# Queueing the resident w2 loads behind the streamed loads, holding eight normalised MLP tiles, and loading the first pair's w1 among the transposes

## Chip, core and metric

The kernel runs on one NeuronCore of one Trainium2 chip. The metric is the device time of one execution in microseconds (us). A matmul instruction here multiplies a 128x128 stationary tile by a 128x512 moving tile; TensorE is called PE, VectorE DVE, ScalarE ACT, GpSimd POOL, and SyncE, which issues the DMAs that matter here, SP.

## Reference

One layer of a hybrid encoder block on x of 1024 tokens by 1024 channels in float32. Only its last part is touched by the change:

```python
x = x + mix @ w_out                                   # 1024x1024
h2 = rms_norm(x, norm_mlp)
x = x + jnp.square(jax.nn.relu(h2 @ w_ff1)) @ w_ff2   # w_ff1 1024x4096, w_ff2 4096x1024
return rms_norm(x, norm_final)
```

## The kernel before

Each float32 factor is split into a high part (ACT casts it, names ending in hi) and the remainder (DVE subtracts, names ending in lo), and a product is three matmuls, hi by hi, hi by lo and lo by hi (`mm3`, L114). Both MLP products use a seven-product scheme of Strassen's kind: the operands are cut into quarters, sums of quarters are formed, and seven products of half size replace eight. The scheme's left operands have the names A11, A12, A22, S1, S2, S3, S4.

The order of the work around the change is this.

**The w_out stage** (L755 to L805). The 8 token tiles are taken in 4 pairs. A pair has four PSUM accumulators `pw` (two tiles, two column halves) of 24 matmuls each; the first pair runs over all four accumulators for each of the 8 row tiles of w_out, the later pairs finish one accumulator after the other. There are four PSUM banks with this tag, so a pair takes the banks of the pair before it. For each token tile DVE adds the accumulator to the residual `x2`, ACT squares the sum and adds up (`square_sum`, L111), POOL raises to the power -1/2 (`rstd`, L108), and DVE scales `x2` into the normalised tile `hn` (L786). The square's elementwise output is written into `hn` and never read. `hn` has 6 buffers for 8 tiles. The `x2` tiles are also stored to DRAM (`x2_d`, L783).

**The transposes.** Tiles 0 to 3 are transposed on PE into `h2t` (L137). Tiles 4 to 7 are combined with tiles 0 to 3 into four `parts` of five operands (L799 to L805), which `transpose_parts` (L815) transposes, four 128x128 blocks each, into PSUM tiles `pt`; ACT and DVE split each of them into `s_hi` and `s_lo`. Among the transposes, `ff1_lead` (L887) does the first two products for column pairs 0, 1 and 2 of w_ff1, since they need `h2t` alone.

**The first MLP product**, 16 pairs g (`ff1`, L892): each loads two blocks of w_ff1 (`raw`), POOL forms four differences from them (`ta`, `tb`), ACT and DVE split them, PE does seven products of 12 matmuls, and the results are combined, squared and stored to DRAM as seven operands (`aops`).

**The second MLP product**, seven products (`product2`, L983) of 16 steps k with 12 matmuls each, in the order A12, A11, S1, S2, S3, A22, S4. A step loads its left operand from DRAM (the streamed load, L992) and its part of w_ff2 by `b_of`. For A12 and A22 that part is streamed as well; for A11, S1 and S2 it goes into resident tiles `r1`, `r2`, `r3` (48 loads of 256 KB, L975), which later products reuse after a subtraction on DVE.

The order of instructions on each engine is chosen by the framework's scheduler; the program can add edges to it. `issue_after(ins)` adds an edge to `ins` from each instruction in its block that runs on the same engine as `ins`:

```python
with tc.issue_after(steps[-1 - AHEAD]) if len(steps) > AHEAD else nullcontext():   # L993
    b = b_of(k, raw[:, 1])
...
    steps[-1] = nc.scalar.copy(out=hi[:, 0], in_=raw[:, 0]).ins                    # L1001, on ACT
```

Here `steps` holds casts on ACT, while `b_of` issues DMAs on SP and subtractions on DVE.

Of the kernel before, what the change touches and what calls it, by code (L numbers as in the profile page):

```python
# [8 lines left out]
F32 = mybir.dt.float32  # L9
# [38 lines left out]
def hybrid_block_kernel(ctx, tc, x, norm_mix, w_in, w_gate_up, b_gate_up, gla_norm, w_proj_sb, w_proj_gla,  # L48
# [717 lines left out]
    for t2 in range(NT // 2):  # L766
# [10 lines left out]
        for tt in (2 * t2, 2 * t2 + 1):  # L777
            hn = hp.tile([P, D], F32, tag="hn", name="hn", bufs=6)
            sums = small.tile([P, 2], F32, tag="ss2", name="sums")
            for ch, sl in enumerate(col_halves):  # L780
                add(x2[tt][:, sl], accs[(tt % 2) * 2 + ch], x2[tt][:, sl])
                square_sum(hn[:, sl], x2[tt][:, sl], sums[:, ch:ch + 1], D)
            nc.sync.dma_start(out=x2_d[tt], in_=x2[tt])  # L783
            r = rstd_of(sums, 2)
            for ch, sl in enumerate(col_halves):
                nc.vector.scalar_tensor_tensor(out=hn[:, sl], in0=x2[tt][:, sl], scalar=r, in1=g_mlp[ch],  # L786
                                               op0=ALU.mult, op1=ALU.mult)
            hns.append(hn)
            if tt < 4:
                load_x2(tt + 4)  # L790
        if t2 == 1:
            ha, hb = (big.tile([P, 4, KT, P], F32R, tag=f"big_{t}0", name=f"h2t_{t}") for t in ("hi", "lo"))
            for tt in range(4):
                transpose_hl((hns[tt][:, c_lo], hns[tt][:, c_hi]),
                             lambda kg: (ha[:, tt, kg * 4:kg * 4 + 4, :], hb[:, tt, kg * 4:kg * 4 + 4, :]), ("tr", "fill"), 2)
        for tt in range(2 * t2, 2 * t2 + 2):
            if tt < 4:
                continue
            h0, h1 = hns[tt - 4], hns[tt]  # L799
            st = hp.tile([P, D], F32, tag="st", name="st", bufs=2)  # L800
            add(st[:, c_lo], h1[:, c_lo], h1[:, c_hi])
            sub(st[:, c_hi], st[:, c_lo], h0[:, c_lo])
            sub(h0[:, c_lo], h0[:, c_lo], h1[:, c_lo], nc.gpsimd)
            sub(h0[:, c_hi], h0[:, c_hi], st[:, c_hi])
            parts.append((st[:, c_hi], h0[:, c_lo], st[:, c_lo], h1[:, c_hi], h0[:, c_hi]))  # L805
# [86 lines left out]
    def ff1(g):  # L892
# [8 lines left out]
        def temp(tag, pool, shape=(P, HALF), bufs=1):  # L901
            return pool.tile(list(shape), F32, tag=tag, name=tag, bufs=bufs)
# [7 lines left out]
        c = lead[g] if g < LEAD else ff1_first(g, pair((b11, b21)))  # L910
# [3 lines left out]
        ta = temp("ta", sop, (P, 2, 4, P))  # L914
        sub(ta[:, 1], b12, b11, nc.gpsimd)
        sub(ta[:, 0], b22, ta[:, 1], nc.gpsimd)
        t2_, t1_ = pair((ta,))
        tb = temp("tb", sop, (P, 2, 4, P))
        sub(tb[:, 0], b22, b12, nc.gpsimd)
        sub(tb[:, 1], b21, ta[:, 0], nc.gpsimd)  # L920
        add(u2, product(t2_, "S2"), u2)
        pc = product(t1_, "S1")
        p5 = temp("p5", sop)
# [3 lines left out]
        u3 = temp("u3", sop)  # L927
# [15 lines left out]
        s2 = temp("s2", fp, bufs=2)  # L943
# [5 lines left out]
        s4 = temp("s4", fp)  # L949
# [5 lines left out]
    transpose_parts((0, 1))  # L955
    ff1_lead(1)
# [22 lines left out]
    AHEAD = 4  # L979
    n_ring = 0  # L980
    steps = []

    def product2(n, o, b_of, tail=False):  # L983
# [3 lines left out]
        for k in range(NK):  # L987
            steps.append(None)
# [3 lines left out]
            nc.sync.dma_start(out=raw[:, 0], in_=aops[o][k])  # L992
            with tc.issue_after(steps[-1 - AHEAD]) if len(steps) > AHEAD else nullcontext():  # L993
                b = b_of(k, raw[:, 1])
            hi = pool.tile([P, 2, HALF], F32R, tag="whi", name="whi", bufs=2)
            lo = pool.tile([P, 2, HALF], F32R, tag="wlo", name="wlo", bufs=2)
            if b is None:
                steps[-1] = nc.scalar.copy(out=hi, in_=raw).ins  # L998
                sub(lo, raw, hi.bitcast(F32))
            else:  # L1000
                steps[-1] = nc.scalar.copy(out=hi[:, 0], in_=raw[:, 0]).ins  # L1001
# [45 lines left out]
    u, v = (xf.tile([P, 4, HALF], F32, name=t) for t in ("u", "v"))  # L1047
# [22 lines left out]
    for i in range(4):  # L1070
        nc.scalar.copy(out=u[:, i], in_=p1[i])
# [7 lines left out]
    for i in range(4):  # L1079
        add(u[:, i], p6[i], u[:, i])  # L1080
        add(x3[i][:, c_hi], u[:, i], x3[i][:, c_hi])
    g_fin = load_g(norm_final)
    p7 = product2(4, "S3", t3x)
    for i in range(4):
        add(u[:, i], p7[i], u[:, i])
        add(v[:, i], u[:, i], v[:, i])
        for sl, src in ((c_hi, v), (c_lo, u)):
            add(x3[4 + i][:, sl], src[:, i], x3[4 + i][:, sl])
# [51 lines left out]
```

## Time and profile before

| what | value |
|---|---|
| median of 3 runs | 1714.35 us (1713.69 to 1715.68) |
| the profiled execution, its own time | 1714.85 us |
| its span in the profile | 1713.1 us |
| PE busy | 1654.5 us (97%) |
| DVE, ACT, POOL busy | 1147.2, 760.5, 388.9 us |
| moved by DMA | 193.54 MB, mean 113 GB/s |
| mean granted PE clock | 0.988 of 2.4 GHz |

The profile shows one execution. Its timeline lists instructions of an engine with start and duration, both in us; a bracket gives how long the engine was idle before and what ended that wait. Durations of matmuls overlap, since they are pipelined, so the pace is read from start to start. The windows view gives, for stretches of time, the busy time of the engines with the count of instructions, the granted PE clock (1.00 is 2.4 GHz), the mean busy share of the 16 DMA engines and their GB/s. In the DMA queue's timeline (SPq) a row is a run of issues by one line.

### The profile page before, as it was taken

The page shows a single profiled execution, that of the slowest core. Times are in us where ns is not written, and L with a number is a line of the kernel's source. Part 1 is how long each engine was busy: PE and PEld are TensorE (multiplying, and loading weights), DVE is VectorE, ACT ScalarE, POOL GpSimd, SP SyncE. Part 2 cuts the span into 40 slices and gives each one's busy share as a digit, 9 for nine tenths or more (in the row PEclk, how much of TensorE's full clock was granted, in tenths as well). Part 3 has the DMA queues.
Part 4 walks back from the last instruction along what each step waited for, and adds up shares of the span by engine and source line. Part 5 has one row for each costly group of instructions (what it writes and reads, how often), then busy time and mean ns, then how long its engine had stood idle before and what let it go on. Part 6 is the DMA issues. An engine that isn't in the chain of part 4 may idle for free.

```text
span 1713.1 us, 22677 instructions
## 1 busy us (share of the span) xinstructions
PE 1654.5 (97%) x8160; PEld 1380.8 (81%) x8160; DVE 1147.2 (67%) x1951; ACT 760.5 (44%) x1545; POOL 388.9 (23%) x380
## 2 busy tenths in 40 slices
PE   7999999999999999999999999899999987999997
PEld 5788888888898888788887787688888866888886
DVE  7678576674624878778856545787776646965695
ACT  6556454564424656557554313222222224444454
POOL 4010000000010121111110011797777520000061
PEclk9999999999999999999999999999999998999999
DMA  7003013032111110116336621454444596333453
GB/s 213 25 20 109 27 49 94 19 91 70 31 62 50 56 54 16 41 58 185 105 130 220 228 79 62 137 164 160 142 142 161 176 389 232 98 98 94 136 166 128
DMA packets 152912, 193.54 MB, mean 113 GB/s; under 512 B 11696, under 2 KB 90544, under 8 KB 152800
## 3 DMA queue, kind: packets, MB, share of 16 engines
q1 hardware_dynamic: 149424, 189.31, 34.6%
q10 hardware_dynamic: 3376, 2.79, 0.5%
q8 instruction: 64, 1.05, 0.3%
q14 instruction: 48, 0.39, 0.1%
HBM read 137.53 MB, written 54.53 MB: 112 GB/s over the span
## 4 chain that ended last, share of the span: by engine, by line
PE 85%; DMA 7%; DVE 4%; ACT 2%; issue 1%; POOL 1%; SPq 0%; ACTq 0%; POOLq 0%; DVEq 0%
PE mmt L115 7%; PE mmt L117 7%; PE mmt L116 7%; PE pq L115 6%; PE pq L116 6%; PE pq L117 6%; PE pp L116 5%; PE pp L115 5%; PE pp L117 5%; PE mmn L116 4%; PE mmn L117 4%; PE mmn L115 4%; PE sc L408 2%; DMA r<-in_w_ff_dram 2%; PE pw L115 2%; PE pw L117 2%
## 5 line engine op out<-in xcount | busy, mean ns | idle before, releaser
L117 PE MATMUL mmt<-ht_hi,wlo 128*128 128x512 f32 x512 | 201.4, 393 | 2.7 <-DVE wlo L79 2.7
L115 PE MATMUL mmt<-ht_hi,whi 128*128 128x512 f32 x512 | 201.6, 394 | 1.3 <-DVE qs L543 1.3
L116 PE MATMUL mmt<-ht_lo,whi 128*128 128x512 f32 x512 | 201.1, 393 | 0.0
L108 POOL TENSOR_TENSOR rstd<-ms,mhalf 128x1 f32<-128x1 f32 x56 | 43.1, 773 | 637.4 <-DVE ms L104 420.4
L115 PE MATMUL pp<-whi 128*128 128x512 f32 x448 | 164.2, 393 | 15.2 <-ACT whi L998 15.2
L116 PE MATMUL pp<-wlo,whi 128*128 128x512 f32 x448 | 176.6, 394 | 0.2
L117 PE MATMUL pp<-whi,wlo 128*128 128x512 f32 x448 | 175.4, 392 | 0.0
L749 DVE TENSOR_TENSOR wlo<-raw,whi 128x512 fp32r<-128x512 f32 (+1 forms) x112 | 89.0, 795 | 96.8 <-ACT whi L1001 53.9
L79 DVE TENSOR_TENSOR wlo<-raw,whi 128x1024 fp32r<-128x1024 f32 (+1 forms) x111 | 122.2, 1102 | 43.8 <-ACT whi L76 43.3
L76 ACT CAST whi<-raw 128x1024 fp32r<-128x1024 f32 (+1 forms) x113 | 95.9, 860 | 114.4 <-PE pq L116 34.7
L116 PE MATMUL mmn<-wlo,ht_hi 128*128 128x512 f32 (+1 forms) x384 | 138.8, 362 | 1.9 <-POOL wlo L79 1.5
L115 PE MATMUL mmn<-whi,ht_hi 128*128 128x512 f32 (+1 forms) x384 | 139.3, 364 | 0.4 <-DVE kl L558 0.4
L117 PE MATMUL mmn<-whi,ht_lo 128*128 128x512 f32 (+1 forms) x384 | 138.6, 361 | 0.0
L115 PE MATMUL pq<-s_hi,whi 128*128 128x512 f32 x320 | 127.4, 398 | 6.6 <-ACT whi L76 6.6
L116 PE MATMUL pq<-s_lo,whi 128*128 128x512 f32 x320 | 126.4, 395 | 0.0
L117 PE MATMUL pq<-s_hi,wlo 128*128 128x512 f32 x320 | 126.2, 395 | 0.0
L1001 ACT CAST whi<-raw 128x512 fp32r<-128x512 f32 x96 | 59.8, 623 | 134.0 <-PE pp L117 110.8
L117 PEld LDWEIGHTS mmt<-ht_hi,wlo 128*128 128x128 f32 x512 | 96.2, 188 | 22.0 <-DVE wlo L79 3.3
L115 PEld LDWEIGHTS mmt<-ht_hi,whi 128*128 128x128 f32 x512 | 96.3, 188 | 20.0 <-issue 1.7
L115 PEld LDWEIGHTS pp<-whi 128*128 128x128 f32 x448 | 84.1, 189 | 34.8 <-ACT whi L998 17.5
L116 PEld LDWEIGHTS mmt<-ht_lo,whi 128*128 128x128 f32 x512 | 96.3, 188 | 18.6
L116 PEld LDWEIGHTS pp<-wlo,whi 128*128 128x128 f32 x448 | 85.0, 190 | 20.2 <-DVE wlo L749 2.7
(261 smaller groups left out, 4024.2 us busy)
## 6 DMA issues: line engine op xcount, KB each, us to landing
raw<-in_w_in_dram SPq DMA_DIRECT2D x36, 512.0 KB, 4.0
raw<-in_w_ff_dram SPq DMA_DIRECT2D x35, 512.0 KB, 4.3
raw<-aop_S SPq DMA_DIRECT2D x64, 256.0 KB, 2.6
aop_A<-c SPq DMA_DIRECT2D x48, 256.0 KB, 3.0
aop_S<-s SPq DMA_DIRECT2D x48, 256.0 KB, 2.2
raw<-aop_A SPq DMA_DIRECT2D x48, 256.0 KB, 2.8
r<-in_w_ff_dram SPq DMA_DIRECT2D x48, 256.0 KB, 5.4
raw<-in_w_in_dram SPq DMA_DIRECT2D x32, 256.0 KB, 3.4
```

The source lines that it names most:

```text
L76: nc.scalar.copy(out=hi, in_=src)
L79: lo_eng.tensor_tensor(out=lo, in0=src, in1=hi.bitcast(F32), op=ALU.subtract)
L108: rstd_ins.append(nc.gpsimd.tensor_tensor(out=r, in0=ms, in1=mhalf, op=ALU.pow).ins)
L115: nc.tensor.matmul(ps, lhsT=sh, rhs=mh, start=first, stop=False)
L116: nc.tensor.matmul(ps, lhsT=sh, rhs=ml, start=False, stop=False)
L117: nc.tensor.matmul(ps, lhsT=sl, rhs=mh, start=False, stop=last)
L408: nc.tensor.matmul(sc[:P - H, i * 64:(i + 1) * 64], lhsT=lev[H][:, j, :P - H], rhs=right, start=True, stop=True)
L749: eng.tensor_tensor(out=out, in0=in0, in1=in1, op=ALU.subtract)
L1001: steps[-1] = nc.scalar.copy(out=hi[:, 0], in_=raw[:, 0]).ins
```

## The change

It has three parts.

1. In `product2` the block around `b_of` is now queued behind the streamed load of the same step, which is on SP.
2. All eight normalised tiles are held at once, in other places: tiles 0, 1, 4, 5 in `hn` (4 buffers), tiles 2 and 3 in the buffers `a21` and `s1` of the pool `fp`, which is opened earlier, and tiles 6 and 7 in `x2` itself, in place, after its store. The squares are written into the accumulators `pw` instead of `hn`. The five operands of a part are formed with three subtractions and one addition that overwrite their inputs, with different engines. The tile `u` of the second product moves into `fp` too.
3. The loads and the weight differences of a pair are a function of their own (`ff1_prep`), and that of pair 0 stands after the transposes of parts 0 and 1; the pool `hp` is closed there, and the second pool of load buffers (`s2`) is opened there.

```diff
+    fp = ctx.enter_context(tc.tile_pool(name="fp", bufs=1))
...
+    def norm_tiles(tt):
+        if tt >= 6:
+            return [x2[tt][:, sl] for sl in col_halves]
+        if tt in (2, 3):
+            return [fp_half("a21"), fp_half("s1")]
+        hn = hp.tile([P, D], F32, tag="hn", name="hn", bufs=4)
+        return [hn[:, sl] for sl in col_halves]
...
-            hn = hp.tile([P, D], F32, tag="hn", name="hn", bufs=6)
             sums = small.tile([P, 2], F32, tag="ss2", name="sums")
             for ch, sl in enumerate(col_halves):
                 add(x2[tt][:, sl], accs[(tt % 2) * 2 + ch], x2[tt][:, sl])
-                square_sum(hn[:, sl], x2[tt][:, sl], sums[:, ch:ch + 1], D)
+                square_sum(accs[(tt % 2) * 2 + ch], x2[tt][:, sl], sums[:, ch:ch + 1], D)
+            hn = norm_tiles(tt)
             nc.sync.dma_start(out=x2_d[tt], in_=x2[tt])
...
-            st = hp.tile([P, D], F32, tag="st", name="st", bufs=2)
-            add(st[:, c_lo], h1[:, c_lo], h1[:, c_hi])
-            sub(st[:, c_hi], st[:, c_lo], h0[:, c_lo])
-            sub(h0[:, c_lo], h0[:, c_lo], h1[:, c_lo], nc.gpsimd)
-            sub(h0[:, c_hi], h0[:, c_hi], st[:, c_hi])
+            st = hp.tile([P, HALF], F32, tag="st", name="st", bufs=2) if tt < 6 else fp_half("s2")
+            sub(h0[0], h0[0], h1[0])
+            sub(st, h1[1], h0[0])
+            add(h1[0], h1[0], h1[1], nc.vector if tt < 6 else nc.gpsimd)
+            sub(h0[1], h0[1], st)
...
+    def ff1_prep(g):
         raw = []
         for kh in range(2):
             raw.append(ring([P, 4, 2 * P], F32, "raw"))
...
+        w1 = pair((b11, b21)) if g >= LEAD else None
+        ta = temp("ta", (P, 2, 4, P))
+        sub(ta[:, 1], b12, b11, nc.gpsimd)
+        sub(ta[:, 0], b22, ta[:, 1], nc.gpsimd)
+        wt = pair((ta,))
+        tb = temp("tb", (P, 2, 4, P))
+        sub(tb[:, 0], b22, b12, nc.gpsimd)
+        sub(tb[:, 1], b21, ta[:, 0], nc.gpsimd)
+        return w1, wt, tb, b22
...
     ff1_lead(0)
     transpose_parts((0, 1))
+    hp_stack.close()
+    pools2.append(ctx.enter_context(tc.tile_pool(name="s2", bufs=1)))
+    n_st = [1, 1]
+    ready = ff1_prep(0)
     ff1_lead(1)
     transpose_parts((2,))
     ff1_lead(2)
     transpose_parts((3,))
-    hp_stack.close()
-    pools2.append(ctx.enter_context(tc.tile_pool(name="s2", bufs=1)))
-    with tc.tile_pool(name="fp", bufs=1) as fp:
-        for g in range(NF // 2):
-            ff1(g)
+    for g in range(NF // 2):
+        ff1(g, *(ready if g == 0 else ff1_prep(g)))
...
-            nc.sync.dma_start(out=raw[:, 0], in_=aops[o][k])
-            with tc.issue_after(steps[-1 - AHEAD]) if len(steps) > AHEAD else nullcontext():
+            load = nc.sync.dma_start(out=raw[:, 0], in_=aops[o][k]).ins
+            with tc.issue_after(load):
                 b = b_of(k, raw[:, 1])
```

What this does to the order, at three places. **The first** is SP's queue in the second MLP product. Before, in the middle of the product A12 (`raw<-aop` and `raw<-in_w_ff` are the two streamed loads of a step, `r` the resident ones, `x` a reload of the residual):

```order
L992 DMA raw<-aop_A_10281 128x512
L975 DMA raw<-in_w_ff_dram 128x512
L975 DMA r_12861<-in_w_ff_dram 128x512 x5
L975 DMA r_12862<-in_w_ff_dram 128x512 x8
L975 DMA r_12863<-in_w_ff_dram 128x512 x4
L992 DMA raw<-aop_A_10281 128x512
L975 DMA raw<-in_w_ff_dram 128x512
L975 DMA r_12863<-in_w_ff_dram 128x512 x3
```

Now, at the end of A12 and the beginning of A11:

```order
L1007 DMA raw<-aop_A_10284 128x512
L993 DMA raw<-in_w_ff_dram 128x512
L1007 DMA raw<-aop_A_10283 128x512
L993 DMA r_12857<-in_w_ff_dram 128x512
L1007 DMA raw<-aop_A_10283 128x512
L993 DMA r_12857<-in_w_ff_dram 128x512
```

All 48 resident loads stood among the steps of A12 and the end of the first MLP product; now each stands right behind the streamed load of its own step in A11, S1 or S2.

The eight reloads of the residual (512 KB each, `x`), which `b_of` issues too, have moved in the same way, from A12 into A11 and S3.

**The second** is the first pair of the w_out stage, on ACT, and the matmul on PE that opens the first accumulator of the second pair. ACT before (`whi<-raw` splits the first two blocks of w_ff1):

```order
L76 CAST wo_hi_9661<-raw 128x1024 [waits DMAHW3_49]
L76 CAST whi<-raw 128x1024 [waits DMAHW2_49]
L112 ACTIVATE hn,sums<-x_0_9665 128x512 [waits DMAHW4_49,DVE_49]
L76 CAST whi<-raw 128x1024 [waits DMAHW3_49]
L112 ACTIVATE hn,sums<-x_0_9665 128x512 [waits DVE_49]
```

ACT now:

```order
L76 CAST wo_hi_9664<-raw 128x1024 [waits DMAHW3_49]
L76 CAST whi<-raw 128x1024 [waits DMAHW2_49]
L112 ACTIVATE pw,sums<-x_0_9668 128x512 [waits DMAHW4_49,DVE_49]
L112 ACTIVATE pw,sums<-x_0_9668 128x512 [waits DVE_49]
L112 ACTIVATE pw,sums<-x_1_9670 128x512 [waits DMAHW5_49,DVE_49]
L112 ACTIVATE pw,sums<-x_1_9670 128x512 [waits DVE_49]
L76 CAST whi<-raw 128x1024 [waits DMAHW5_49]
```

PE before, the last matmuls of the first pair and the first of the second:

```order
L115 MATMUL pw<-wo_hi_9661,mixt_hi_8921 128x512
L116 MATMUL pw<-wo_lo_9662,mixt_hi_8921 128x512
L117 MATMUL pw<-wo_hi_9661,mixt_lo_8922 128x512
L115 MATMUL pw<-wo_hi_9312,mixt_hi_8921 128x512 [waits DVE_49]
L116 MATMUL pw<-wo_lo_9313,mixt_hi_8921 128x512
```

PE now:

```order
L115 MATMUL pw<-wo_hi_9664,mixt_hi_8921 128x512
L116 MATMUL pw<-wo_lo_9665,mixt_hi_8921 128x512
L117 MATMUL pw<-wo_hi_9664,mixt_lo_8922 128x512
L115 MATMUL pw<-wo_hi_9312,mixt_hi_8921 128x512 [waits Activation_49]
L116 MATMUL pw<-wo_lo_9313,mixt_hi_8921 128x512
```

The cast of the first w_ff1 block stands ahead of the first square in both. The matmul waits for ACT's square where it waited for DVE's addition.

**The third** is PE between the w_out stage and the first pair's own products (`pq<-s`), with the names of the transposed tiles. Before, from the end of the last product of column pair 2 on:

```order
L115 MATMUL pq<-h2t_hi,whi 128x512
L116 MATMUL pq<-h2t_lo,whi 128x512
L117 MATMUL pq<-h2t_hi,wlo 128x512
L822 MATMUL pt<-ident,st 128x128 x4
L822 MATMUL pt<-ident,hn 128x128 x4
L822 MATMUL pt<-ident,st 128x128 x4
L822 MATMUL pt<-ident,hn 128x128 x8
L115 MATMUL pq<-s_hi,whi 128x512
```

Now, around the beginning of the products of column pair 2:

```order
L835 MATMUL pt<-ident,x_6_9924 128x128 x8
L835 MATMUL pt<-ident,s_9916 128x128 x4
L835 MATMUL pt<-ident,s_10265 128x128 x4
L835 MATMUL pt<-ident,x_7_9940 128x128 x4
L115 MATMUL pq<-h2t_hi,whi 128x512
L116 MATMUL pq<-h2t_lo,whi 128x512
L115 MATMUL pq<-h2t_hi,whi 128x512
L116 MATMUL pq<-h2t_lo,whi 128x512
L835 MATMUL pt<-ident,a_9931 128x128 x4
L115 MATMUL pq<-s_hi,whi 128x512
```

The products of column pair 2 (24 matmuls) now stand between the last transposes and the first pair's products, where before five transposes stood directly ahead of them.

## Rows read from the trace of the kernel before

**Rows 1.** Timeline of PE: the waits between the w_out stage and the end.

```profile
1058.37 0.66 PE L822 MATMUL pt<-ident,hn 128*128 128x128 f32 x4 [1.53 <-DVE s_lo L749]
1061.22 1.12 PE L822 MATMUL pt<-ident,hn 128*128 128x128 f32 x4 [2.20 <-DVE s_lo L749]
...
1082.19 0.79 PE L115 MATMUL pq<-s_hi,whi 128*128 128x512 f32 x1 [6.57 <-ACT whi L76]
...
1417.24 2.08 PE L115 MATMUL pp<-whi 128*128 128x512 f32 x4 [10.26 <-ACT whi L998]
...
1430.34 1.25 PE L115 MATMUL pp<-whi 128*128 128x512 f32 x4 [3.82 <-ACT whi L998]
```

**Rows 2.** Timeline of ACT in product A12.

```profile
1416.14 1.04 ACT L998 CAST whi<-raw 128x1024 fp32r<-128x1024 f32 x1 [12.58 <-DMA raw<-in_w_ff_dram]
```

**Rows 3.** Timeline of the DMA queue SPq in product A12.

```profile
1397.70 11.51 SPq L975 DMA_DIRECT2D r<-in_w_ff_dram  x17
1410.03 0.33 SPq L992 DMA_DIRECT2D raw<-aop_A  x1
1410.66 0.33 SPq L975 DMA_DIRECT2D raw<-in_w_ff_dram  x1
```

**Rows 4.** Windows of PE in A12: stretch, length, busy, clock, DMA share, GB/s.

```profile
1377.70:1394.00 16.30, 16.30 (x73) 1.00 1.05 395
1394.00:1437.70 43.70, 28.28 (x98) 0.84 0.97 355
```

**Rows 5.** Timeline of PE: first matmul of A12, and two later steps of it.

```profile
1377.76 0.40 PE L115 MATMUL pp<-whi 128*128 128x512 f32 x1
...
1434.99 1.07 PE L115 MATMUL pp<-whi 128*128 128x512 f32 x4
...
1437.71 1.07 PE L115 MATMUL pp<-whi 128*128 128x512 f32 x4
```

**Rows 6.** Windows, in A11/S1 and during A22's loads: busy of five engines, clock, DMA share, GB/s.

```profile
1450.00:1500.00 50.00, 50.00 (x222) 41.43 (x221) 47.64 (x77) 22.53 (x40) 0.00 (x0) 1.00 0.34 95
...
1600.00:1650.00 50.00, 50.00 (x222) 41.42 (x221) 44.56 (x67) 23.13 (x44) 24.06 (x4) 1.00 0.53 174
```

**Rows 7.** Timelines around the second pair of the w_out stage: PE, DVE, ACT.

```profile
971.51 0.39 PE L115 MATMUL pw<-wo_hi,mixt_hi 128*128 128x512 f32 x1
...
982.91 0.69 DVE L746 TENSOR_TENSOR x<-pw,x 128x512 f32<-128x512 f32 x1 [0.38 <-PE pw L117]
...
973.82 1.05 ACT L76 CAST whi<-raw 128x1024 fp32r<-128x1024 f32 x1 [8.55 <-DMA raw<-in_w_ff_dram]
974.77 0.63 ACT L112 ACTIVATE hn<-x 128x512 f32<-128x512 f32 x1
```

**Rows 8.** Timeline of PE after the w_out stage.

```profile
1042.19 0.39 PE L115 MATMUL pq<-h2t_hi,whi 128*128 128x512 f32 x1
...
1047.66 0.60 PE L822 MATMUL pt<-ident,st 128*128 128x128 f32 x4
1048.10 0.60 PE L822 MATMUL pt<-ident,hn 128*128 128x128 f32 x4
...
1086.85 0.40 PE L115 MATMUL pq<-s_hi,whi 128*128 128x512 f32 x1
```

**Rows 9.** Timeline of DVE, same place.

```profile
1042.39 0.69 DVE L746 TENSOR_TENSOR x<-pw,x 128x512 f32<-128x512 f32 x1 [4.91 <-PE pw L117]
...
1074.22 3.08 DVE L749 TENSOR_TENSOR s_lo<-pt,s_hi 128x512 fp32r<-128x512 f32 x5
```

**Rows 10.** Timelines of SPq and of POOL, same place.

```profile
1075.77 23.15 SPq L896 DMA_DIRECT2D raw<-in_w_ff_dram  x6
...
1079.80 1.26 POOL L749 TENSOR_TENSOR ta<-raw,ta 128x512 f32<-128x512 f32 x1 [12.57 <-DMA raw<-in_w_ff_dram]
...
1089.67 2.28 POOL L749 TENSOR_TENSOR tb<-raw,ta 128x512 f32<-128x512 f32 x1
```

**Rows 11.** The line L783, stores of x2: time from issue to landing.

```profile
DMA to landing us min/median/max: 2.6/2.9/5.6
```

More of the change, by code (lines that the diff above doesn't have):

```diff
@@ L1 @@
-from contextlib import ExitStack, nullcontext
+from contextlib import ExitStack
 import concourse.bass as bass
@@ L785, in hybrid_block_kernel @@
             for ch, sl in enumerate(col_halves):
-                nc.vector.scalar_tensor_tensor(out=hn[:, sl], in0=x2[tt][:, sl], scalar=r, in1=g_mlp[ch],
+                nc.vector.scalar_tensor_tensor(out=hn[ch], in0=x2[tt][:, sl], scalar=r, in1=g_mlp[ch],
                                                op0=ALU.mult, op1=ALU.mult)
@@ L799, in hybrid_block_kernel @@
             h0, h1 = hns[tt - 4], hns[tt]
[L800 to L805 removed]
+            st = hp.tile([P, HALF], F32, tag="st", name="st", bufs=2) if tt < 6 else fp_half("s2")
[3 more added lines that the diff above has]
+            sub(h0[1], h0[1], st)
+            parts.append((st, h0[0], h1[0], h1[1], h0[1]))
     wo_stack.close()
@@ L890, in ff1_lead, with temp @@
         lead.append(ff1_first(g, pair((raw,))))
-    def ff1(g):
+    def temp(tag, shape=(P, HALF)):
+        return sop.tile(list(shape), F32, tag=tag, name=tag)
+    def ff1_prep(g):
         raw = []
@@ L899, in ff1 @@
         b21, b22 = raw[1][:, :, :P], raw[1][:, :, P:]
-        def temp(tag, pool, shape=(P, HALF), bufs=1):
-            return pool.tile(list(shape), F32, tag=tag, name=tag, bufs=bufs)
+        w1 = pair((b11, b21)) if g >= LEAD else None
[7 more added lines that the diff above has]
+        return w1, wt, tb, b22
+    def ff1(g, w1, wt, tb, b22):
         def relu_sq(c):
@@ L908, in store @@
             nc.sync.dma_start(out=aops[o][g], in_=c)
-        c = lead[g] if g < LEAD else ff1_first(g, pair((b11, b21)))
+        c = lead[g] if g < LEAD else ff1_first(g, w1)
         a11, u2 = c[:, 0], c[:, 1]
@@ L913, in ff1 @@
         store("A11", a11)
[L914 to L923, printed above, removed]
+        add(u2, product(wt[0], "S2"), u2)
+        pc = product(wt[1], "S1")
+        p5 = temp("p5")
         nc.scalar.copy(out=p5, in_=pc)
@@ L997, in product2 @@
             if b is None:
-                steps[-1] = nc.scalar.copy(out=hi, in_=raw).ins
+                nc.scalar.copy(out=hi, in_=raw)
                 sub(lo, raw, hi.bitcast(F32))
             else:
-                steps[-1] = nc.scalar.copy(out=hi[:, 0], in_=raw[:, 0]).ins
+                nc.scalar.copy(out=hi[:, 0], in_=raw[:, 0])
                 sub(lo[:, 0], raw[:, 0], hi[:, 0].bitcast(F32))
@@ L1045, in t4 @@
         return at(r1, k)
-    u, v = (xf.tile([P, 4, HALF], F32, name=t) for t in ("u", "v"))
+    u = [fp_half(t) for t in ("a21", "s1") for _ in range(2)]
+    v = xf.tile([P, 4, HALF], F32, name="v")
     xh = xf.tile([P, 4, D], F32, name="x3_0")
@@ L1070, in hybrid_block_kernel @@
     for i in range(4):
-        nc.scalar.copy(out=u[:, i], in_=p1[i])
+        nc.scalar.copy(out=u[i], in_=p1[i])
         add(v[:, i], p1[i], v[:, i])
@@ L1079, in hybrid_block_kernel @@
     for i in range(4):
-        add(u[:, i], p6[i], u[:, i])
-        add(x3[i][:, c_hi], u[:, i], x3[i][:, c_hi])
+        add(u[i], p6[i], u[i])
+        add(x3[i][:, c_hi], u[i], x3[i][:, c_hi])
     g_fin = load_g(norm_final)
@@ L1084, in hybrid_block_kernel @@
     for i in range(4):
[L1085 to L1088, printed above, removed]
+        add(u[i], p7[i], u[i])
+        add(v[:, i], u[i], v[:, i])
+        for sl, src in ((c_hi, v[:, i]), (c_lo, u[i])):
+            add(x3[4 + i][:, sl], src, x3[4 + i][:, sl])
     def finish(tt, acc, ch):
```

19 lines of the change are left out of this document (9 added, 10 removed).

## Prediction

> **What bounds the kernel now.** PE is busy 97% of the span, so I looked first, in the list of who waited for whom, at the little that PE waits. PE's timeline puts nearly all of it in two places [rows 1]. Between the w_out stage and the first MLP product there are waits of 1.53, 2.20 and 6.57 us (and two of 0.4); in the product A12 there are waits of 10.26 and 3.82 us (and one of 1.1). The reader should see that the gaps are few and large, and that everything between them is PE at full clock. A change elsewhere gains nothing unless it lets PE start something sooner.
>
> In A12 the chain goes PE, ACT, DMA. PE waits for the cast `whi`; ACT's row at 1416.14 says that ACT had itself waited 12.58 us for `raw<-in_w_ff` [rows 2]; and the queue shows why that load was late: SP issued 17 resident loads from 1397.70 on, and only then, at 1410.03 and 1410.66, the next streamed pair [rows 3]. Meanwhile the DMA engines were full, 395 and 355 GB/s at a busy share near 1 [rows 4]. So a stretch of traffic that nobody needs yet holds up traffic that PE needs now.
>
> At the first place PE's 6.57 us end with the cast of `ta`. POOL had waited 12.57 us for the load of w_ff1 [rows 10], which SP could issue only at 1075.77, when the last transposes had freed its memory.
>
> **Resident loads (part 1): a gain of 21.0 us.** A step of A12 is 12 matmuls and takes 2.72 us at full pace (1434.99 to 1437.71) [rows 5]. The step that begins at 1437.71 is the fifteenth: the windows count 73 + 98 = 171 matmuls from 1377.70 to 1437.70 [rows 4], 14 steps of 12 and a few that straddle an edge. Fourteen steps after 1377.76 would end at 1415.8; they end 21.9 us later. Of this 15.2 us are the three waits, the rest matmuls at the lower clock (0.84 granted on average [rows 4]) and weights that come just in time. With the 17 loads gone each step needs two loads of 256 KB in 2.72 us, 193 GB/s, half of what was moved here. I take 21.0 and keep 0.9 for first steps that may come late. The bounds are 21.9 and, if a third wait like the 3.82 us stays, 18.
>
> The loads do not vanish. A11, S1 and S2 now carry 512 KB a step instead of 256, and A11 also four reloads of 512 KB. What hides that is the pattern of A22, which has both loads in each step: while they run, PE is busy 50.00 of 50 us at 174 GB/s [rows 6]. If that cover failed, the price is the rival below. DVE's subtractions for S1, S2 and S3 can no longer run far ahead. In the new order S2 has four DVE operations of 512 columns in a step, 64 in 43.5 us; DVE already did 77 in 50 us, 47.64 us busy, with PE never idle [rows 6]. That is the same rate (1.47 and 1.54 a us), so it costs nothing, though little is left over.
>
> **Squares into the accumulators (part 2): a loss of 5.5 us.** This adds a wait. The second pair's first matmul starts at 971.51; the addition at 982.91, which waited for the end of the second accumulation, confirms it (48 matmuls of 0.233 us before 982.7) [rows 7]. Now it waits for ACT's square of the first accumulator. That square stands on ACT behind the cast of the first w_ff1 block, which started at 973.82 after waiting 8.55 us for its load [rows 7]. Before, the square was just as late, but nobody waited for it. The cast takes 1.05 us, the square starts at 974.77 and takes 0.63, so PE starts at about 975.5: 4.0 us lost. The following accumulations find their squares done, since each takes 5.6 us. The load should not come sooner, since the same loads stand ahead of it in SP's queue.
>
> After such a pause matmuls run slow for a while: after the pause of 6.57 us eleven matmuls took 4.66 us (1082.19 to 1086.85 [rows 1, 8]) instead of 2.57, a loss of 2.1; starts 0.42 us apart instead of 0.23 belong to the lower of the clock's two levels, 1.2 GHz. PE was dense before this pause, so 0 is the other end; I take 1.5, nearer to the row. Bounds of the term: 0 (the load comes earlier) and 8.
>
> **Eight tiles and the early w1 (parts 2 and 3): a gain of 9 us.** I walk through PE's new order on before's clock. The w_out stage ends at 1042.19, the first lead products at 1047.66 [rows 8]. The normalisation of tiles 6 and 7 no longer waits for buffers, but in place it waits for the store: the last addition ends at 1043.1 [rows 9], the store lands 2.9 us later [rows 11], and two scalings (0.7 each) and four other DVE operations of 0.7 stand before the first `s_lo`, which comes at about 1051 and is then followed by one every 0.62 us [rows 9]. PE has three transposes, twelve matmuls and seven more transposes to do, four blocks in 0.44 us [rows 8]; with four PSUM buffers they end at `s_lo`'s pace, at 1055.5, some 1 us of it waiting. Then the second w_ff1 block can be loaded, 4.0 us (1075.77 to 1079.80 [rows 10]), to 1059.5. Three subtractions on POOL at 1.26 us [rows 10] lead to `ta` at 1063.3, and two casts of 1.05 us on ACT (that of `ta`, and behind it that of column pair 2) to 1065.4. PE, out of transposes at about 1063.5, waits for the second cast some 2 us. The 24 matmuls of column pair 2 and three transposes, 5.5 + 1.3 us, fill PE to 1072.3, and then the first pair's own products are ready. Before, they started at 1082.19 with 2.1 us of slow matmuls, as good as 1084.3. The difference is 12.0. I subtract 3.0 for the low clock, since thin stretches of transposes with waits precede here too, as they did before 1062. The ceiling is PE without any gap: 72 matmuls of 0.2275 and 20 transposes of 0.44 end at 1067.4, a gain of 16.9. The floor is 3: the load comes later and the first pair then waits for POOL.
>
> POOL's price decides part of this. Alone, a subtraction took 1.26 us at 1079.80; beside a DVE subtraction it took 2.28 at 1089.67 [rows 10]. In the new order the three subtractions run beside DVE's `s_lo`, whose first input is in PSUM. I take 1.26; at 2.28 the path is 3.1 us longer. The Trainium skill (SBUF — State Buffer, "Who interferes with whom") says that a DVE instruction contends with a GpSimd instruction that reads SBUF when it has two SBUF inputs, and not with one; by that rule `s_lo` does no harm and the sum stays as it is, and by a rule without that exception it would be 3.1 us more. The row at 1089.67 agrees with the first half.
>
> **Sum.** -21.0 + 5.5 - 9.0 = -24.5 us. The profiled execution took 1714.85 us, 0.5 above the median; 1714.35 - 24.5 gives 1689.9, so I predict 1690. About 0.2%, 3.4 us, is what a measurement of this kernel can tell from no change.
>
> **Rivals.** (a) The streamed and the resident load together are too much for A11, S1 and S2. SP issues in order, so a streamed load that waits for its buffer holds the resident load behind it, and DVE and ACT then wait for that. A12 under pressure lost 21.9 us in 14 steps [rows 4, 5], 1.56 a step, at 355 to 395 GB/s; at 193 GB/s I charge half of that, 0.78, and 48 steps lose 37 us, more than all gains: 1727. It decides from 24.5/48 = 0.51 us a step. Against it stands A22 [rows 6]: chance 0.05. (b) The first place only changes what it waits for: POOL, ACT or the store in place is as late as the transposes were, and the 9 us shrink to nothing: 1699. Chance 0.16. For it speaks how many things now meet there. (c) The pause in the w_out stage does not come, the w_ff1 load being early enough: 1684.5. Chance 0.12. (d) POOL's subtractions take 2.28 us beside any DVE work: 1693. Chance 0.10. (e) Part 1 does not do what it says. The new order shows the loads moved, so 0.02; then 1711. (f) The gains come near their bounds (21.9 and 13) and the pause costs 1: 1680.5, chance 0.05. My forecast has the remaining 0.50.
>
> **Range and chances.** From 1680 (f) to 1702 (b with the lower bound of part 1, 18): this leaves out (a), (e) and some tails, less than 2 in 10. Faster by over 0.2%: all cases but (a) and (e), 0.93. Within: (e) and the weak end of (a), 0.03. Slower: 0.04.
>
> **What would show it.** In the profile after: no wait of PE above 1 us in A12 and steps of 2.7 us from its first matmul on; the resident loads spread over three products at some 190 GB/s, with PE busy throughout; a new wait of about 4 us for ACT in the w_out stage, ended by `pw` being squared, behind a cast that waited for w_ff1; about 30 us from the end of the w_out stage to the first pair's own products, instead of 40. The forecast is wrong if PE waits in A11, S1 or S2, or if the first pair starts no earlier after the w_out stage than before.

## The result and the profile after

The changed kernel takes 1686.78 us (median of 4 runs, 1685.91 to 1690.64), the kernel before beside it 1714.84: a ratio of 0.9841, 95% interval 0.9824 to 0.9858. The profiled execution took 1686.03 us. The forecast was 1690, in a range of 1680 to 1702. In a later comparison on the chip the ratio was 0.9847 (0.9828 to 0.9867).

The page of the changed kernel says that PE is busy for 98% of a span of 1684.3 us, and its rows of the second MLP product have no idle time ahead of them:

```profile
PE 1645.4 (98%) x8160; PEld 1376.9 (82%) x8160; DVE 1145.9 (68%) x1953; ACT 761.8 (45%) x1545; POOL 383.0 (23%) x378
...
L115 PE MATMUL pp<-whi 128*128 128x512 f32 x448 | 165.7, 389 | 0.0
```

PE's timeline, cut to the marks of the stages and every wait of 0.3 us or more after 950 us (start, duration, engine, line; in brackets the idle time before and what ended it):

```profile
945.04 0.40 PE L115 MATMUL pw<-wo_hi,mixt_hi 128*128 128x512 f32 x1
...
967.83 0.39 PE L117 MATMUL pw<-wo_hi,mixt_lo 128*128 128x512 f32 x1
972.70 0.53 PE L115 MATMUL pw<-wo_hi,mixt_hi 128*128 128x512 f32 x1 [4.48 <-ACT pw L112]
...
976.45 0.40 PE L115 MATMUL pw<-wo_hi,mixt_hi 128*128 128x512 f32 x1
...
1044.80 0.39 PE L117 MATMUL pw<-wo_hi,mixt_lo 128*128 128x512 f32 x1
...
1063.99 0.66 PE L835 MATMUL pt<-ident,s 128*128 128x128 f32 x4 [0.37 <-DVE s_lo L749]
1065.18 0.66 PE L835 MATMUL pt<-ident,s 128*128 128x128 f32 x4 [0.54 <-DVE s_lo L749]
1066.42 0.63 PE L835 MATMUL pt<-ident,x 128*128 128x128 f32 x4 [0.58 <-issue]
1069.00 0.79 PE L115 MATMUL pq<-h2t_hi,whi 128*128 128x512 f32 x1 [1.95 <-ACT whi L76]
...
1370.77 0.40 PE L115 MATMUL pp<-whi 128*128 128x512 f32 x1
```

Set against [rows 1], the waits of 10.26 and 3.82 us in A12 and that of 6.57 us ahead of the first pair are gone, and there is one new large wait, 4.48 us in the w_out stage.

I cut the span at three marks that every kernel has: the first matmul into `pw`, the last one, and the first into `pp` (the start of A12). This gives four stretches for each profiled run. The table holds all runs of this study; "ratio" is to the kernel before in the same comparison, and only the first stretch has nothing of the change in it.

| run | median us | ratio (95%) | to first pw | w_out stage | to A12 | A12 to end |
|---|---|---|---|---|---|---|
| before | 1714.84 | 1 | 948.23 | 93.73 | 335.80 | 335.34 |
| after | 1686.78 | 0.9841 (0.9824 to 0.9858) | 945.04 | 99.76 | 325.97 | 313.53 |
| p1_only | 1690.14 | 0.9865 (0.9847 to 0.9883) | 945.26 | 93.63 | 334.70 | 313.51 |
| no_p1 | 1707.83 | 0.9978 (0.9965 to 0.9991) | 945.79 | 99.09 | 326.03 | 334.99 |
| ahead4 | 1689.28 | 0.9857 (0.9835 to 0.9879) | 948.69 | 101.12 | 326.18 | 313.51 |
| extra_load | 1695.88 | 0.9899 (0.9872 to 0.9926) | 946.55 | 101.09 | 326.37 | 320.79 |
| sq_norm | 1681.45 | 0.9814 (0.9797 to 0.9831) | 947.53 | 93.58 | 324.45 | 313.54 |
| cast_behind | 1682.18 | 0.9817 (0.9798 to 0.9837) | 946.68 | 93.47 | 327.40 | 313.55 |
| late_w1 | 1683.83 | 0.9827 (0.9810 to 0.9845) | 946.41 | 99.45 | 323.56 | 313.58 |
| tiles_swapped | 1691.08 | 0.9878 (0.9847 to 0.9908) | 944.91 | 99.12 | 331.81 | 313.56 |
| lead2_first | 1683.98 | 0.9834 (0.9813 to 0.9856) | 946.04 | 99.87 | 322.97 | 313.52 |
| sq_late | 1677.41 | 0.9792 (0.9774 to 0.9810) | 943.25 | 93.46 | 323.53 | 313.56 |
| sq_lead2 | 1679.23 | 0.9798 (0.9778 to 0.9818) | 948.44 | 93.31 | 322.86 | 313.59 |
| after_again | 1687.85 | 0.9847 (0.9828 to 0.9867) | 945.38 | 99.25 | 327.48 | 313.49 |

From before to after the stretches change by -3.19, +6.03, -9.83 and -21.81 us. The first is no effect of the change: over the runs it lies between 943.25 and 948.69 with the same instructions there. The other three add to -25.6, where the forecast had -24.5. So the 3 us by which the median lies below 1690 are mostly that first stretch, and in the later comparison the change was -25.8 us (1713.63 to 1687.85).

For part 1, the windows of the changed kernel, one for each product from A12 to S2 or nearly so (busy us and instructions of PE, PEld, DVE, ACT, POOL; then the granted clock, the DMA engines' busy share and GB/s):

```profile
1370.00:1414.00 44.00, 44.00 (x195) 36.37 (x195) 23.77 (x22) 18.20 (x22) 7.93 (x4) 1.00 0.72 233
1414.00:1458.00 44.00, 44.00 (x196) 36.44 (x195) 24.10 (x38) 20.65 (x37) 0.00 (x0) 1.00 0.70 228
1458.00:1502.00 44.00, 44.00 (x196) 36.44 (x195) 37.85 (x62) 20.64 (x37) 0.00 (x0) 1.00 0.61 191
1502.00:1546.00 44.00, 44.00 (x195) 36.42 (x195) 36.99 (x61) 19.25 (x35) 0.00 (x0) 1.00 0.59 182
```

PE is busy throughout at full clock; the 395 GB/s of [rows 4] have become 182 to 233. SP's queue in A11 shows why: one streamed and one resident load every 2.7 us, in place of the run of 17 in [rows 3].

```profile
1421.34 0.32 SPq L1007 DMA_DIRECT2D raw<-aop_A  x1
1421.71 0.43 SPq L993 DMA_DIRECT2D r<-in_w_ff_dram  x1
1424.06 0.32 SPq L1007 DMA_DIRECT2D raw<-aop_A  x1
1424.42 0.43 SPq L993 DMA_DIRECT2D r<-in_w_ff_dram  x1
```

### The profile page after: what moved, and what is told of

Its sections match the earlier page's. It is cut to its first block, busy times and chain, and to the rows that moved or that the text cites. A ratio compares the mean times of both kernels' runs of the same rounds, so it can differ in the third digit from the quotient of the medians.

```text
span 1684.3 us, 22683 instructions
## 1 busy us (share of the span) xinstructions
PE 1645.4 (98%) x8160; PEld 1376.9 (82%) x8160; DVE 1145.9 (68%) x1953; ACT 761.8 (45%) x1545; POOL 383.0 (23%) x378
## 4 chain that ended last, share of the span: by engine, by line
PE 88%; DMA 4%; DVE 4%; ACT 2%; issue 1%; POOL 1%; SPq 0%; ACTq 0%; POOLq 0%; DVEq 0%
PE mmt L117 7%; PE mmt L115 7%; PE mmt L116 7%; PE pq L115 6%; PE pp L115 6%; PE pp L116 6%; PE pp L117 6%; PE pq L117 6%; PE pq L116 6%; PE mmn L116 4%; PE mmn L117 4%; PE mmn L115 4%; PE sc L408 2%; PE pw L115 2%; PE pw L117 2%; PE pw L116 2%
## 5 line engine op out<-in xcount | busy, mean ns | idle before, releaser
L117 PEld LDWEIGHTS pp<-whi,wlo 128*128 128x128 f32 x448 | 84.1, 188 | 17.5
```

The source lines that it names most:

```text
L117: nc.tensor.matmul(ps, lhsT=sl, rhs=mh, start=False, stop=last)
```

## The experiments

**Part 1 alone, and all but part 1.** The theory was that part 1 gives back what A12 lost, whatever else is done. `p1_only` puts the new edge into the kernel before, `no_p1` the old one into the changed kernel. This is the edit of `no_p1`, without the lines that keep `steps`:

```diff
-            load = nc.sync.dma_start(out=raw[:, 0], in_=aops[o][k]).ins
-            with tc.issue_after(load):
+            nc.sync.dma_start(out=raw[:, 0], in_=aops[o][k])
+            with tc.issue_after(steps[-1 - AHEAD]) if len(steps) > AHEAD else nullcontext():
```

> The kernel before with the first part of the change alone (the resident loads queued behind the streamed load of their step). Theory: the part's worth does not depend on the others, so it gives what the product A12 and all that follows lost, 21 to 22 us: about 1693 us, no wait of PE above 1 us in A12, the waits of 1.53, 2.20 and 6.57 us ahead of the first MLP product still there. Rival: the second and third part also relieve A12 (they let SP reach it with a shorter queue), so alone it gives 15 us or less: 1700 us or more.

> The changed kernel with the old edge behind casts on ACT. Theory: the loss in A12 comes back whole, 21 to 22 us: about 1708.5 us, with PE waits of some 10 and 4 us in A12, and 17 or so resident loads in one run on SP's queue. Rival: with A12 starting 7 us earlier and other loads ahead of it the burst falls elsewhere: 1703 us or less.

`p1_only` took 1690.14 us, 22.0 less than the kernel before beside it, and its last stretch 313.51, the same as in the changed kernel. PE waited nowhere after the start of A12, and for 6.67 us ahead of the first pair. `no_p1` took 1707.83, and its last stretch is 334.99, 21.5 longer than after. There PE waited 16.0 us in A12, the longest time 10.49, behind a run of 17 resident loads:

```profile
1413.91 2.07 PE L115 MATMUL pp<-whi 128*128 128x512 f32 x4 [10.49 <-ACT whi L1016]
...
1424.56 1.20 PE L115 MATMUL pp<-whi 128*128 128x512 f32 x4 [2.58 <-ACT whi L1016]
```

```profile
1392.90 13.46 SPq L993 DMA_DIRECT2D r<-in_w_ff_dram  x17
```

The first fence is PE's timeline of `no_p1`, the second SP's queue. Both theories held: part 1 is worth 21.5 to 22 us alone, and does not depend on the rest.

**Is it the distance, or the engine of the edge?** `ahead4` keeps the edge on SP but puts it four steps back, the distance that the old edge had:

```diff
+            loads.append(load)
-            with tc.issue_after(load):
+            with tc.issue_after(loads[-1 - AHEAD]) if len(loads) > AHEAD else nullcontext():
```

> The changed kernel with the resident load queued behind the streamed load of four steps before, on SP, in place of the same step. Theory: the old edge failed since it stood behind casts on ACT and so did not bind SP's loads; an edge on SP with the same distance of four steps lets only some four loads pass, which A12's steps have room for: within 2 us of the changed kernel. Rival: the distance itself is the fault; loads let ahead delay the streamed pair and PE waits in A12 as before, 5 us or more: 1690 us.

The last stretch took 313.51 us, and PE waited nowhere in it; the total of 1689.28 has an interval that overlaps with that of the changed kernel in the same comparison. The old edge was written with a distance of four steps too, but from a cast on ACT, and `issue_after` ties only instructions on the same engine. It named no instruction of SP, so it held back no load.

**How much traffic do A11, S1 and S2 bear?** Rival (a) of the prediction said that two loads a step would be too much. The change itself, at 182 to 228 GB/s in these products, lost nothing, so `extra_load` adds a third load (its data is not used) to each of the 48 steps, here for A11 and in the same way for S1 and S2:

```diff
         load_b(at(r1, k), 0, 0, k)
+        load_b(fp_half('s2'), 0, 0, k)
```

> The changed kernel with a third load of 256 KB in each of the 48 steps of A11, S1 and S2 (the resident block a second time, into a tile that nobody reads): 12 MB more, 289 GB/s in these steps in place of 193. Theory: what hurt A12 was the run of loads ahead of the streamed pair in SP's queue, not the rate, so with the order kept PE stays busy: under 2 us more than the changed kernel, 1685 to 1687 us. Rival, the prediction's case of too much traffic: the steps lose 0.5 us or more each, 24 us in all: 1709 us.

Neither was right. The last stretch grew by 7.3 us. PE's timeline holds three waits after the start of A12; these are the two large ones:

```profile
1472.15 0.50 PE L116 MATMUL pp<-wlo,whi 128*128 128x512 f32 x1 [1.84 <-DVE wlo L79]
...
1519.27 0.80 PE L116 MATMUL pp<-wlo,whi 128*128 128x512 f32 x1 [2.35 <-DVE wlo L79]
```

The windows of the same run (A11, then two that hold S1 and S2):

```profile
1414.00:1458.00 44.00, 44.00 (x196) 36.44 (x195) 20.37 (x33) 20.24 (x36) 0.00 (x0) 1.00 0.92 321
1458.00:1502.00 44.00, 42.16 (x187) 34.58 (x186) 33.65 (x55) 20.04 (x35) 0.00 (x0) 1.00 0.80 262
1502.00:1546.00 44.00, 41.35 (x173) 33.12 (x172) 38.14 (x62) 19.06 (x34) 0.00 (x0) 0.96 0.80 258
```

A11 had the highest rate, 321 GB/s at a share of 0.92, and PE lost nothing there. The loads did come later: a resident load issued between 1408 and 1446 took a median of 6.3 us to land, against 3.8 in the changed kernel, and DVE stood 4.67 us for the first block of S1 (0.81 in the changed kernel):

```profile
1451.59 0.69 DVE L749 TENSOR_TENSOR r<-r,r 128x512 f32<-128x512 f32 x1 [4.67 <-DMA r<-in_w_ff_dram]
```

S1 and S2 lost time at a lower rate. What differs in the rows is DVE: there the resident block is first an operand of a subtraction, and ACT's cast and the split wait for it. DVE's row before the first wait, and ACT's:

```profile
1466.00 0.69 DVE L749 TENSOR_TENSOR r<-r,r 128x512 f32<-128x512 f32 x1 [1.53 <-DMA r<-in_w_ff_dram]
1466.61 2.48 DVE L746 TENSOR_TENSOR v<-pp,v 128x512 f32<-128x512 f32 x4
```

```profile
1471.53 0.62 ACT L76 CAST whi<-r 128x512 fp32r<-128x512 f32 x1 [1.42 <-DVE r L749]
```

A late block stops DVE, and then the additions at the end of the product stand ahead of the next subtraction. So the rate alone did not stop PE. Loads came late, and a late load cost time only where DVE, with little room, stood between it and PE. This is read from the rows; no run tests it apart. The third load also had only two buffers, for which SP waited 14.7 us in A11, so part of the lateness may be its own. That the late blocks are the whole of the 7.3 us was not shown either: the three waits make 4.4, and the lower clock in the last window some of the rest.

**The pause in the w_out stage.** The prediction had it behind ACT's square, and that behind a cast that waits for a load. ACT's timeline of the changed kernel:

```profile
970.98 1.04 ACT L76 CAST whi<-raw 128x1024 fp32r<-128x1024 f32 x1 [9.33 <-DMA raw<-in_w_ff_dram]
971.93 0.59 ACT L112 ACTIVATE pw<-x 128x512 f32<-128x512 f32 x1
```

Two kernels remove it in different ways. `sq_norm` writes the squares somewhere else, and PE then needs none of them; `cast_behind` leaves them in the accumulators and queues the cast behind them.

```diff
-                square_sum(accs[(tt % 2) * 2 + ch], x2[tt][:, sl], sums[:, ch:ch + 1], D)
-            hn = norm_tiles(tt)
+                square_sum(hn[ch] if tt < 6 else accs[(tt % 2) * 2 + ch], x2[tt][:, sl], sums[:, ch:ch + 1], D)
```

(with `hn = norm_tiles(tt)` ahead of the loop), and

```diff
-        lead.append(ff1_first(g, pair((raw,))))
+        with tc.issue_after(first_squares):
+            w = pair((raw,))
+        lead.append(ff1_first(g, w))
```

> The changed kernel with the squares of tiles 0 to 5 written into the buffers of the normalised tiles (only those of tiles 6 and 7 into the accumulators). Theory: the wait of 4.5 us for ACT's square in the w_out stage and the slow matmuls behind it go, together 6.3 us, and nothing else there is late: about 1680.5 us, granted clock 1.00 from 960 us to the end of the w_out stage. Rival 1: the wait moves to another late thing (the cast of the first w_ff1 block, which waits for its DMA): 1686 us. Rival 2: the stretch after the w_out stage hangs on loads and stores that do not come earlier with PE and gives half back: 1683.5 us.

> The changed kernel, squares in the accumulators, with the casts of the first product's blocks of column pairs 0 to 2 queued behind the squares of tiles 0 and 1 on ACT. Theory: PE waited for the square only since it stood behind a cast that waited for its DMA; DVE's additions of tile 0 end at 967.6, so the squares are done by about 968.3 and PE, done with the first pair at 967.8, waits under 1 us: some 6 us less than the changed kernel, as with the squares put elsewhere, 1680 to 1682 us. Rival: the square in PSUM is itself late or slow there and 3 us or more of the wait stay: 1684 us.

(`first_squares` is the last square of tiles 0 and 1.) Both brought the w_out stage back to 93.5 us, 6.2 less than after, with no wait of PE in its later pairs: 1681.45 and 1682.18 us. ACT's timeline of `cast_behind` has the order turned round:

```profile
968.53 0.60 ACT L112 ACTIVATE pw<-x 128x512 f32<-128x512 f32 x1 [4.75 <-DVE x L746]
...
972.52 1.05 ACT L76 CAST whi<-raw 128x1024 fp32r<-128x1024 f32 x1 [1.17 <-DMA raw<-in_w_ff_dram]
```

So the square in PSUM was not late in itself. It stood behind a cast that nobody needed for another 70 us.

**Is it the early preparation, or the tiles?** The prediction gave one sum for both. `late_w1` moves the preparation of pair 0 back behind all transposes and keeps the tiles. Without the line on `n_st` it also changes buffers: pair 0's first block and column pair 2's weights then go into the older pool of load buffers, no longer into the new one.

```diff
-    hp_stack.close()
-    pools2.append(ctx.enter_context(tc.tile_pool(name="s2", bufs=1)))
-    n_st = [1, 1]
-    ready = ff1_prep(0)
     ff1_lead(1)
     transpose_parts((2,))
     ff1_lead(2)
     transpose_parts((3,))
+    hp_stack.close()
+    pools2.append(ctx.enter_context(tc.tile_pool(name="s2", bufs=1)))
+    ready = ff1_prep(0)
```

> The changed kernel with the loads and weight differences of pair 0 back behind all transposes (tiles and squares stay as changed). Theory: the eight tiles alone only let PE reach the same wait sooner; the second block of w_ff1 can be issued only after the last transposes, some 1073 us on the changed kernel's clock, then 4 us of load, 3.9 us of subtractions on POOL and a cast of 1 us, so PE stands 7 to 9 us and runs slow for 2: 1694 to 1697 us. Rival: the tiles were most of the 9.8 us and the early load little: 1689 us or less.

It fell far from my expectation: the stretch to A12 took 323.56 us, 2.4 less than after, not 8 more. SP's queue, POOL and ACT of `late_w1`:

```profile
1056.22 6.83 SPq L912 DMA_DIRECT2D raw<-in_w_ff_dram  x3
```

```profile
1066.18 1.50 POOL L749 TENSOR_TENSOR ta<-raw,ta 128x512 f32<-128x512 f32 x1 [12.27 <-DMA raw<-in_w_ff_dram]
```

```profile
1051.54 1.05 ACT L76 CAST whi<-raw 128x1024 fp32r<-128x1024 f32 x1 [1.91 <-PE pq L116]
...
1067.71 1.05 ACT L76 CAST whi<-ta 128x1024 fp32r<-128x1024 f32 x1 [1.07 <-POOL ta L749]
```

The load was early although it is written late: the run of three issues ends at 1063, and the block that POOL waits for is issued in it at 1062.1, well before the last transposes (1075.95). It waits only until the memory it goes to is free. In the changed kernel `hp` holds tiles 0, 1, 4 and 5, which the transposes of parts 0 and 1 use up, and the framework lets the load follow the last reader of those tiles, not the place where the pool is closed. `tiles_swapped` tests that with one line, on top of `late_w1`: as many tiles are held, but `hp` has tiles 2 to 5, so that part 3 still needs it.

```diff
-        if tt in (2, 3):
+        if tt in (0, 1):
```

> As the run with pair 0's preparation written behind all transposes, but tiles 0 and 1, not 2 and 3, lie in the halves a21 and s1, so that the pool hp holds tiles 2 to 5 and is in use until the transposes of part 3. All else is the same, the number of tiles held too. Theory: the load of w_ff1 became early because the memory under it held only tiles of parts 0 and 1, wherever the program writes the load; so now SP issues it only after the last transposes, some 1072 us, and PE waits 6 to 8 us for the cast of ta as before the change: 1691 to 1694 us. Rival: the gain comes from normalised tiles that no longer wait for a buffer, and the place of the memory counts little: 1686 us or less.

The stretch took 331.81 us, 8.25 more than `late_w1`, and 1691.08 in all. Its rows on SP, POOL and PE are again like those of the kernel before [rows 1, 10]:

```profile
1071.73 15.99 SPq L912 DMA_DIRECT2D raw<-in_w_ff_dram  x5
```

```profile
1077.43 1.26 POOL L749 TENSOR_TENSOR ta<-raw,ta 128x512 f32<-128x512 f32 x1 [25.36 <-DMA raw<-in_w_ff_dram]
```

```profile
1079.83 0.80 PE L115 MATMUL pq<-s_hi,whi 128*128 128x512 f32 x1 [8.12 <-ACT whi L76]
```

Which tiles lie under the load's buffer is thus worth 8.25 us. Against the 334.70 of `p1_only`, which has neither, 2.9 us remain for the rest of part 2 (eight tiles held, the operands of a part formed in place); this second difference is small, since two profiles of the changed kernel differ by 1.5 us in this stretch (325.97 and 327.48).

**What the early preparation costs.** In `late_w1` ACT casts column pair 2's weights at 1051.54, ahead of `ta`. In the changed kernel the cast of `ta` stands ahead of it, since it is written earlier, and PE waits 1.95 us for pair 2's at 1069.00. `lead2_first` keeps the early preparation but writes that cast of `ta` behind the lead product of pair 2:

```diff
-        wt = pair((ta,))
+        wt = None if g == 0 else pair((ta,))
...
     ff1_lead(2)
+    n_st[0] += 1
+    ready = (ready[0], pair((ready[1],)), *ready[2:])
```

(`n_st` starts at `[2, 1]`, so that the buffers are the same ones, and `ff1_prep` returns `ta` where it has no `wt`).

> The changed kernel with the cast of ta, pair 0's first difference, written behind the lead product of column pair 2, so that ACT casts that pair's weights first. Theory: the run with the preparation written late was 2.4 us shorter from the end of the w_out stage to the product A12, because there this cast stood ahead of ta's; so the wait of 1.95 us and its slow matmuls go and 2.4 us are gained against the changed kernel, at 0.984 of the kernel before: about 1682.5 us. Rival: the difference came from the loads of the second pair, which this leaves as they are: no gain, 1685 us.

ACT's timeline of `lead2_first`:

```profile
1060.53 1.05 ACT L76 CAST whi<-raw 128x1024 fp32r<-128x1024 f32 x1
1068.14 1.05 ACT L76 CAST whi<-ta 128x1024 fp32r<-128x1024 f32 x1 [2.73 <-POOL ta L749]
```

The wait of 1.95 us is gone, and the stretch took 322.97 us, 3.0 less than after and 4.5 less than `after_again`. The totals (ratios 0.9834 and 0.9847, with intervals that overlap) are too close to tell, so the gain is shown by the stretch alone. There it holds over all runs of the table: the four in which pair 2's weights are cast before `ta` lie between 322.86 and 323.56 us, the seven with the early preparation as the change has it between 324.45 and 327.48. Since `lead2_first` keeps the buffers, the order of the casts is enough for it.

**The two improvements together.** `sq_late` is `sq_norm` and `late_w1` in one, `sq_lead2` is `sq_norm` and `lead2_first`; `after_again` is the control in the last comparison.

> Both improvements together: squares of tiles 0 to 5 in the buffers of the normalised tiles, and pair 0's preparation written behind all transposes. Theory: they act in different stretches, so their gains add, 6.2 us and 2.4 us in the stretches against the changed kernel: about 1679 us, faster than any run so far. Rival: the early end of the w_out stage takes the cover from the loads that the late order needs, and it is no better than the squares alone: 1681.5 us.

> Squares in the buffers of the normalised tiles and the cast of column pair 2 ahead of that of ta, with the early preparation of pair 0 kept. Theory: the stretch from the end of the w_out stage to A12 was 322.97 us with this order and 323.56 us with the late preparation, so this is 0.6 us better than the fastest run so far: ratio 0.979 to the kernel before, 1676 to 1678 us. Rival: without the pause in the w_out stage the stores and loads of this order come too late and it is 2 us or more slower than that run.

> The changed kernel itself, for comparison within one call: ratio 0.984 to the kernel before as in the first measurement, 1685 us where the kernel before takes 1712 us.

`sq_late` took 1677.41 us, ratio 0.9792 (0.9774 to 0.9810), below the interval of the changed kernel (0.9828 to 0.9867). `sq_lead2`, 0.9798 (0.9778 to 0.9818), can't be told from it: their three last stretches add to 730.55 and 729.76 us, against 739.26 after. The gains of `sq_late` add, 8.7 us where 6.2 and 2.4 were expected; `sq_lead2` missed the 1676 to 1678 us that I expected, at 1679.23. Either beats both kernels.

## Why the prediction was right

**Resident loads: -21.0 forecast, -21.8 in the profiles, -22.0 and -21.5 in the two runs that isolate it.** The count of 14 steps that ended 21.9 us late [rows 4, 5] was the whole of it; the 0.9 that I kept back was not needed. PE waits nowhere in A12, and SP's streamed loads in A11 are issued 2.72 us apart (1421.34 and 1424.06), the full pace of a step. The cover held as A22 had shown, DVE included (62 operations in 44 us). Rival (a) was priced too high: `extra_load`, with half as much traffic again, lost 0.15 us a step, not 0.78, and it came in S1 and S2, where DVE has work on the block, not where the rate was highest. What it named as the end of the chain, DVE and ACT waiting for a late resident load, is in those rows.

**Squares: +5.5 forecast, +6.03 measured.** The mechanism was named in full: the load, the cast, the square, PE. From 967.83 to 972.70 PE lost 4.6 us (forecast 4.0), and the nine matmuls from there to 976.45 took 3.75 us instead of 2.1, so 1.65 (forecast 1.5). That is the lower of the clock's two levels, as the starts 0.42 apart say. The window over these nine shows it as a granted clock of 0.55:

```profile
972.70:976.40 3.70, 3.70 (x9) 2.92 (x10) 3.03 (x6) 1.90 (x6) 0.55 (x1) 0.55 0.46 135
```

Over the eight profiled kernels with this pause the stage took 99.09 to 101.12 us, 5.4 to 7.4 more than before. The low end of this term, 0 because PE was dense before the pause, did not come, and neither did rival (c), a stage without the pause.

**Eight tiles and early w1: -9 forecast, -9.83 measured** (-8.3 with the second profile of the changed kernel). The walk can be checked row by row; the w_out stage ended 2.84 us later than on before's clock. These are DVE, SP and POOL in that stretch of the changed kernel:

```profile
1049.40 1.42 DVE L799 SCALAR_TENSOR_TENSOR x<-x,rstd,g_row 128x512 f32<-128x512 f32 x2 [2.47 <-DMA x_d<-x]
...
1053.91 0.68 DVE L749 TENSOR_TENSOR s_lo<-pt,s_hi 128x512 fp32r<-128x512 f32 x1
```

```profile
1058.93 0.93 SPq L912 DMA_DIRECT2D raw<-in_w_ff_dram  x2
```

```profile
1062.98 1.48 POOL L749 TENSOR_TENSOR ta<-raw 128x512 f32<-128x512 f32 x1 [10.14 <-DMA raw<-in_w_ff_dram]
1064.43 1.27 POOL L749 TENSOR_TENSOR tb<-raw 128x512 f32<-128x512 f32 x1
1065.65 1.27 POOL L749 TENSOR_TENSOR ta<-raw,ta 128x512 f32<-128x512 f32 x1
```

The scaling in place waits for its store; the first `s_lo` was forecast at 1051 + 2.84 and came at 1053.91; the load was forecast to land at 1062.3 and ended POOL's wait at 1062.98; PE's wait for the cast was put at some 2 us and was 1.95. So rival (b), that the place only changes what it waits for, fell. The price of POOL was the lower one: the second and third subtraction took 1.27 us beside `s_lo` (DVE's `s_lo` run from 1063.25 to 1066.3), so rival (d) fell as well. The prediction had drawn a rule from the Trainium skill (SBUF — State Buffer, "Who interferes with whom"), that a DVE operation with one SBUF input does not contend with GpSimd; these rows agree with it.

**What was right by sum only.** Two steps of this walk were off by about 1 us each. The terms for the first `s_lo` add to 1050.2 (1043.1, 2.9 and six operations of 0.7), not to the 1051 written down; in the trace the store held the scaling back until 1049.40, 3.5 us after the last addition, and 4.5 us of DVE work followed, so the figure came right by luck. And the 3.0 us subtracted for the low clock were too much. PE started on column pair 2 at 1069.00, 0.8 later than forecast, and needed 8.0 us from there to the first pair's own products, where the walk had 6.8:

```profile
1076.99 0.48 PE L116 MATMUL pq<-s_lo,whi 128*128 128x512 f32 x1
```

That is 2.0 of the 3.0; the slow stretch up to 1072.10 lost some 1.5 of it (five matmuls and a transpose of four blocks in 3.1 us, where 1.6 is the full pace). One matmul of those products ran earlier, at 1071.58. From the end of the w_out stage this is 32 us, where the forecast said about 30.

The term was one number for two parts, and the step that read the early load as part 3's doing, "Then the second w_ff1 block can be loaded", was not taken apart. The runs take it apart: 8.25 us from which tiles share memory with the load and some 3 from the rest of part 2. Part 3 takes 2.4 to 3.0 back by putting the cast of `ta` ahead of the one that PE needs first. Nothing in the forecast's total depended on this, but a reader who took from it that the load must be *written* earlier would have kept the wrong half of the edit.

**A reading that was too wide.** The prediction has nearly all of PE's waiting in two places. That is so only from the w_out stage to the end of the products. In the whole span PE was idle for 58.6 us before the change (1713.1 less 1654.5), and the waits listed there are 26.2 of them. It did no harm to the sum, since the change was priced at these places alone.

## What to carry to other kernels

An ordering edge like `issue_after` holds back only the engine it is on: to keep bulk loads from running ahead of loads that are needed now, tie them to a DMA on the same queue, and look at the queue's rows to see whether the edge did anything. Here a load started when the last reader of the memory beneath it was done, wherever it was written, so choose which tiles lie there, and test the place of the code and the place of the memory apart. When an unread result is put into a buffer that another engine wants back, look at what the writer's queue has ahead of it: here a cast that waited for a DMA cost 6 us, and one edge or another buffer took it away.

## What the runs showed of the hardware

I had not expected that DMA traffic at 321 GB/s and a busy share of 0.92 would leave PE busy for 44.00 of 44 us (`extra_load`, A11) with loads that took 6.3 us to land, while 258 GB/s in the same run, with loads that landed in 3.3 us, did not, where the blocks pass through DVE first. And a single pause of 4.48 us in a stretch that was dense before and after put PE on the lower clock level for nine matmuls, 1.65 us on top of the pause; the wait of 1.95 us at 1069.00 was also followed by starts 0.42 us apart, until 1072.10, at a granted clock of 0.51. Waits of 0.4 to 0.6 us among the transposes, just ahead of it, stand in the same stretch, so which of them weighed was not tested.
